# Moving a kernel's SBUF-to-DRAM-to-SBUF bounces from GpSimd's DMA queue to SyncE's, and estimating their loads as parallel

## The chip, the cores and the metric

The kernel runs on one core of a Trainium2 chip. The metric is device time in microseconds of one execution; three runs of the kernel before gave 746.6, 746.7 and 748.06 us, median 746.7. A core has five engines, each with an instruction order of its own: TensorE (PE, with its weight loads as PEld), VectorE (DVE), ScalarE (ACT), GpSimd (POOL) and SyncE (SP). Any of the last three can issue a DMA; an engine works through its instructions in order, so one that waits holds up those behind it.

## What is computed

Two decoder layers over a sequence of 256 tokens with 1024 features, in float32. Each layer is a token mixer with two attention branches, then a SwiGLU feed-forward, each followed by a layer norm over the scaled residual. Cut to its frame:

```python
def hybrid_mixer(x, w_in, w_branch_sb, w_branch_moba, w_out):
    proj = x @ w_in
    q_sb, k_sb, v_sb, q_mb, k_mb, v_mb, g_sb, g_mb = jnp.split(proj, cuts, axis=-1)
    o_sb = stick_breaking_attention(...)                       # 8 heads of 64
    o_mb = moba_attention(partial_rope(q_mb), partial_rope(k_mb), v_mb)   # 8 heads of 64
    merged = sigmoid(g_sb) * (o_sb @ w_branch_sb) + sigmoid(g_mb) * (o_mb @ w_branch_moba)
    return merged @ w_out

def swiglu(x, w_gate, w_up, w_down):                           # D_FF = 2816
    return (silu(x @ w_gate) * (x @ w_up)) @ w_down

for l in range(2):
    x = layer_norm(ALPHA * x + hybrid_mixer(x, ...))
    x = layer_norm(ALPHA * x + swiglu(x, ...))
```

With 256 tokens MoBA's block is the whole sequence, so that branch is causal softmax attention.

## The kernel before

**Weights.** They stream through SBUF once, as 2 x 122 granules of 128 x 1024 float32 (512 KB). For accuracy each granule is used as two parts, a rounded high part and the rest (`whi`, `wlo`), and each product is three matmuls (`mm3`: high x high, high x low, low x high, line 423; `mm` issues them at line 417). The parts lie in two rings of ten places; a place is free again when TensorE has used the granule ten before (`allow`).

Most granules are loaded by SyncE into one of six raw buffers (`load`, line 135), cast by ScalarE into `whi`, and subtracted by VectorE into `wlo`, which frees the raw buffer (`line`, lines 149 to 172). Seven granules of each layer (22, 25, 28, 31, 34, 37, 40, "soft") go another way, without VectorE: GpSimd issues a DMA from the weights straight into `whi` (`cast_line`), ScalarE writes the negative of that into `wlo`, and GpSimd issues a second DMA that adds the weights to it (`rest_line`).

**The order of the work.** The program is written out in one pass by a planner, `Weave`. TensorE's matmuls advance an estimated time `weave.t`. Everything else is a generator ("side") that yields the estimated time at which it may go on; after each group of matmuls, `tick` steps every side whose time has come, and what it issues is then next in that engine's order. Three helpers issue an instruction and estimate its end: `act` (line 47), `dve` (line 52), `pool` (line 57). Each holds a clock for its engine: an instruction begins at the later of that clock and `e`, the time at which its input is there, and the helper returns its end plus a hop of 0.21 us. In the trace all instructions that go through a helper carry the helper's line: L48 for ScalarE, L53 for VectorE, L58 for GpSimd. The soft granules' estimated arrival follows from the end that `pool` returns, and so does `ws.dma_t`, the estimate of when the DMA engines are free. These estimates decide only the order; on the chip every instruction waits on semaphores for what it really needs.

**The bounces.** The rotary query and key of the MoBA branch, and the first four feed-forward chunks, are computed with tokens on the partitions but needed with features there. `turned_line` (line 501) turns a 128 x (n x 128) tile: VectorE transposes its 32 x 32 blocks into `half`, one DMA stores `half` to a scratch tensor in DRAM (`scr`, three buffers of each size), and four DMAs load the blocks back rearranged, each into 32 partitions of `out`. The loads wait for the store's landing. With n = 4 (query and key: `l0qmb`, `l0kmb` and so on, two token halves each) a store has 256 KB and a load 64 KB; with n = 2 (`l0sg` into `l0hb`, four each layer) it is half of that. That makes eight bounces, eight stores and 32 loads, in each layer. GpSimd issues all of them. What comes back is split into two parts by ScalarE and VectorE (`split_line`).

**Stages of a layer,** in TensorE's order: MoBA query and stick-breaking value (`l0pv`, `l0pq`; `l1pvq`), query and key of stick-breaking heads (`l0pqk`) around the MoBA key (`l0pk`), MoBA value (`l0pu`), the gates (`l0pg`) with the attention's scores (`l0sb_s`, `l0mb_s`), transposes (`_pT`) and outputs (`_o`) in between, the branch projections (`l0pb`), the output projection (`l0pw`), the norm's transposes (`l0a_tp`), four feed-forward chunks (`l0pft`), the other eighteen (`l0pf`), and the down projection (`l0pd`, in the second layer `l1pd` and `l1pe`).

Of the kernel before, what the change touches and what calls it, by code (L numbers as in the profile page):

```python
# [34 lines left out]
class Weave:  # L35
# [16 lines left out]
    def dve(self, e, n, f, *args, **kw):  # L52
        f(*args, **kw)  # L53
        self.dve_t = max(self.dve_t, e) + n / 960.0 + DVE_FIXED
        return self.dve_t + HOP

    def pool(self, e, f, *args, **kw):
        f(*args, **kw)  # L58
        self.pool_t = max(self.pool_t, e) + 0.3
        return self.pool_t + HOP  # L60

    def add(self, gen, due=0.0, last=False):
# [36 lines left out]
class WeightStream:  # L99
# [5 lines left out]
    def __init__(self, nc, pool, rings, w, total, weave):  # L105
        self.nc, self.pool, self.rings, self.w, self.total, self.weave = nc, pool, rings, w, total, weave
        self.soft = [g for g in range(total) if SOFT(g)]
        self.hard = [g for g in range(total) if not SOFT(g)]
        self.loaded = self.split = self.cast = self.done = 0
        self.limit = NSPLIT - 1  # L110
        self.current = 0
        self.dma_t = 1.7
        self.raw, self.parts, self.there, self.ready = {}, {}, {}, {}
# [140 lines left out]
DMA_STORE = 3.0  # L254
DMA_LOAD = 3.0
# [3 lines left out]
def hybrid_trunk_kernel(ctx: ExitStack, tc: tile.TileContext, w, xT_in, x_in, ln_in,  # L259
                        ident_in, mask_in, rope_in, out):  # L260
    nc = tc.nc
# [54 lines left out]
    act, dve, pool = weave.act, weave.dve, weave.pool  # L316
# [73 lines left out]
    e = dve(3.6, 512, nc.vector.tensor_copy, hi, ws.raw[0][:, first[0]])  # L390
# [110 lines left out]
    def turned_line(name, out, half, src, n, e):  # L501

        scr = dram.tile([P, n * P], F32, tag=f"scr{n}", name=f"{name}_scr")
        e = dve(e, n * P, nc.vector.transpose, half.rearrange("p (j n b) -> p n j b", j=4, n=n),
                src.rearrange("p (n j a) -> p n j a", n=n, j=4))
        yield e
        e = pool(e, nc.gpsimd.dma_start, scr, half) + DMA_STORE
        yield e
        blocks = scr.rearrange("(i a) (j c) -> j a i c", a=32, j=4)
        for j in range(4):  # L510
            e = max(e, pool(e, nc.gpsimd.dma_start, out[32 * j:32 * j + 32].rearrange("a (i c) -> a i c", i=4),
                            blocks[j]) + DMA_LOAD)
        yield e
        return out.rearrange("p (i n b) -> p n i b", i=4, n=n), e

# [3 lines left out]
    def rope_line(name, ps, t, put, scale=1.0):  # L519

        both = unit(f"{name}_tok{t}", [P, 2, WIDTH])
        tmp = both[:, 0, :].rearrange("p (h d) -> p h d", d=DH)
        e = act(pe_done(), WIDTH, nc.scalar.activation, tmp, ps.rearrange("p (h d) -> p h d", d=DH), AF.Copy,
                scale=scale)
        yield e
        half = ROPE // 2
        a, b = (p.tile([P, n], F32, tag=tag, name=f"{name}_{tag}{t}")[:, :8 * ROPE]
                .rearrange("p (h r) -> p h r", h=8) for p, tag, n in ((page1, "ra", 240), (page2, "rb", 208)))
        cc = rope[:, t, 0, None, :].to_broadcast([P, 8, ROPE])
        s0 = rope[:, t, 1, None, :half].to_broadcast([P, 8, half])  # L530
        s1 = rope[:, t, 1, None, half:].to_broadcast([P, 8, half])
        mul = nc.vector.tensor_mul
        dve(e, P, mul, a, tmp[:, :, :ROPE], cc)
        dve(e, P // 2, mul, b[:, :, :half], tmp[:, :, half:ROPE], s0)
        dve(e, P // 2, mul, b[:, :, half:], tmp[:, :, :half], s1)
        e = dve(e, 2 * P, nc.vector.tensor_add, tmp[:, :, :ROPE], a, b)
        tp, e = yield from turned_line(f"{name}{t}", both[:, 0, :], both[:, 1, :], both[:, 0, :], NPAIR, e)
        yield from put(tp, slice(t * P, (t + 1) * P), e)
# [232 lines left out]
    for l in range(DEPTH):  # L771
# [112 lines left out]
        for c, b in ((0, 0), (1, 0), (0, 1), (1, 1), *((c, b) for c in range(2, KC) for b in range(2))):  # L884
# [15 lines left out]
            e = dve(0.0, S, nc.vector.tensor_add, mt[:, 0, :], mt[:, 0, :], mt[:, 1, :])  # L900
# [21 lines left out]
        def h_line(name, ps, j, t):  # L922
            sg = work.tile([P, 256], F32, tag="T", name=name)
            e = act(pe_done(), 256, nc.scalar.activation, sg, ps[:, :256], AF.Sigmoid)
            yield e
            dve(e, 256, nc.vector.tensor_mul, sg, sg, ps[:, :256])
            e = dve(e, 256, nc.vector.tensor_mul, sg, sg, ps[:, 256:])
            tp, e = yield from turned_line(name, hb[t][:, j, 1, :], hb[t][:, j, 0, :], sg, 2, e)
            ts = slice(t * P, (t + 1) * P)
            yield from split_line(*(blocked(h[:, 2 * j:2 * j + 2, ts]) for h in h_t[0]), tp, 256, e)  # L930
# [139 lines left out]
```

## Time and profile before

| what | value |
|---|---|
| median of three runs | 746.7 us (746.6 to 748.06) |
| profiled execution | 745.83 us |
| its span, first to last instruction | 744.0 us |
| PE busy | 718.3 us (97%) |
| PEld busy | 659.5 us (89%) |
| DVE busy | 524.7 us (71%) |
| ACT busy | 391.1 us (53%) |
| POOL busy | 77.9 us (10%), 128 instructions |
| DMA | 149.95 MB, 202 GB/s over the span |
| weight loads issued by SP | 226 of 512 KB, median 4.4 us to landing |
| soft granules' DMAs issued by POOL | 28 of 512 KB, median 4.5 us (high) and 7.4 us (low) to landing |

Times in the profile are microseconds from the span's start. In a timeline row stand start, length, engine, source line, operation, output and inputs, and in brackets how long the engine stood idle before it and what released it. In the list of waits stand the waiting instruction, what it waited for, the sum, the count and the longest. A DMA's row on SP or POOL is its issue; the landing comes later and is listed apart. The granted clock is TensorE's, as a share of full speed.

### The profile page before, as it was taken

The numbers are of one execution on the slowest core, as the hardware profiler recorded it, in microseconds if no ns is written. First come the engines' busy times: TensorE is split into PE (matmuls) and PEld (weight loads), VectorE is DVE, ScalarE is ACT, GpSimd is POOL, SyncE is SP. The second block draws the span as 40 slices with busy tenths as digits, with TensorE's granted clock in tenths as the row PEclk, the third lists the DMA queues.
The fourth block names the chain that finished last, engine by engine and source line by source line (L and its number), as shares of the span: only waits on it lengthen the run. The fifth ranks groups of instructions, "written<-read, shape, count | busy, mean of one in ns | idle before, by whom it ended". The sixth has DMA issues, their size and how long they took to land.

```text
span 744.0 us, 12787 instructions
## 1 busy us (share of the span) xinstructions
PE 718.3 (97%) x5032; PEld 659.5 (89%) x5032; DVE 524.7 (71%) x792; ACT 391.1 (53%) x588; POOL 77.9 (10%) x128
## 2 busy tenths in 40 slices
PE   8996899999999999999999999899999999999995
PEld 6986699998899999988889888799988999998884
DVE  5997568786896766644588887777679766665415
ACT  5756377754565545533356565686346545554300
POOL 0123011000230000000012221100012300000001
PEclk9999799999999999999999999999999999999998
DMA  8997677555597565566259486857636966563501
GB/s 304 357 317 238 154 199 209 183 176 171 200 306 239 189 199 199 171 241 218 72 191 344 159 223 175 214 159 244 195 113 224 314 197 201 182 197 100 230 1 57
DMA packets 45083, 149.95 MB, mean 202 GB/s; under 512 B 5984, under 2 KB 8032, under 8 KB 45024
## 3 DMA queue, kind: packets, MB, share of 16 engines
q1 hardware_dynamic: 37776, 127.91, 50.8%
q0 software_dynamic: 7104, 20.98, 11.7%
q8 instruction: 39, 0.64, 0.3%
q10 hardware_dynamic: 144, 0.26, 0.1%
q14 instruction: 20, 0.16, 0.1%
HBM read 144.93 MB, written 4.19 MB: 200 GB/s over the span
## 4 chain that ended last, share of the span: by engine, by line
PE 93%; ACT 2%; DMA 2%; DVE 2%; issue 0%; POOL 0%; POOLq 0%; SPq 0%; DVEq 0%
PE l1pf L417 13%; PE l0pf L417 13%; PE l0pd L417 8%; PE l0pg L417 6%; PE l1pg L417 6%; PE l1pe L417 4%; PE l1pd L417 4%; PE l1pqk L417 3%; PE l0pw L417 3%; PE l1pw L417 3%; PE l1pft L417 3%; PE l0pft L417 3%; PE l1pvq L417 3%; PE l0pb L417 3%; PE l0pqk L417 3%; PE l1pb L417 2%
## 5 line engine op out<-in xcount | busy, mean ns | idle before, releaser
L53 DVE TENSOR_TENSOR wlo<-raw,whi 128x1024 fp32r<-128x1024 f32 (+1 forms) x234 | 278.3, 1203 | 87.1 <-ACT whi L48 83.9
L48 ACT CAST whi<-raw 128x1024 fp32r<-128x1024 f32 (+1 forms) x233 | 238.4, 1036 | 84.4 <-PE l0pd L417 19.7
L417 PE MATMUL l1pf<-xT_hi,whi 128*128 128x256 f32 x288 | 79.6, 276 | 0.0
L417 PE MATMUL l1pf<-xT_hi,wlo 128*128 128x256 f32 x288 | 79.6, 276 | 0.0
L417 PE MATMUL l1pf<-xT_lo,whi 128*128 128x256 f32 x288 | 79.6, 276 | 0.0
L417 PE MATMUL l0pf<-xT_hi,whi 128*128 128x256 f32 x288 | 79.5, 276 | 0.0
L417 PE MATMUL l0pf<-xT_hi,wlo 128*128 128x256 f32 x288 | 79.5, 276 | 0.0
L417 PE MATMUL l0pf<-xT_lo,whi 128*128 128x256 f32 x288 | 79.5, 276 | 0.0
L417 PEld LDWEIGHTS l1pf<-xT_hi,whi 128*128 128x128 f32 x288 | 54.1, 188 | 0.0
L417 PEld LDWEIGHTS l1pf<-xT_lo,whi 128*128 128x128 f32 x288 | 54.1, 188 | 0.0
L417 PEld LDWEIGHTS l1pf<-xT_hi,wlo 128*128 128x128 f32 x288 | 54.1, 188 | 0.0
L417 PEld LDWEIGHTS l0pf<-xT_hi,whi 128*128 128x128 f32 x288 | 54.1, 188 | 0.0
L417 PEld LDWEIGHTS l0pf<-xT_lo,whi 128*128 128x128 f32 x288 | 54.1, 188 | 0.0
L417 PEld LDWEIGHTS l0pf<-xT_hi,wlo 128*128 128x128 f32 x288 | 54.1, 188 | 0.0
L417 PE MATMUL l1pg<-xT_hi,whi 128*128 128x256 f32 x128 | 36.5, 286 | 1.4 <-DVE l1vmb L53 1.4
L417 PE MATMUL l0pg<-xT_hi,whi 128*128 128x256 f32 x128 | 36.0, 281 | 0.0
L417 PE MATMUL l1pg<-xT_hi,wlo 128*128 128x256 f32 x128 | 35.9, 280 | 0.0
L417 PE MATMUL l1pg<-xT_lo,whi 128*128 128x256 f32 x128 | 35.9, 280 | 0.0
L417 PE MATMUL l0pg<-xT_hi,wlo 128*128 128x256 f32 x128 | 35.5, 277 | 0.0
L417 PE MATMUL l0pg<-xT_lo,whi 128*128 128x256 f32 x128 | 35.4, 277 | 0.0
L417 PE MATMUL l0pd<-whi,l0h_hi 128*128 128x512 f32 x88 | 34.5, 391 | 0.0
L417 PE MATMUL l0pd<-wlo,l0h_hi 128*128 128x512 f32 x88 | 34.3, 389 | 0.0
(359 smaller groups left out, 1841.3 us busy)
## 6 DMA issues: line engine op xcount, KB each, us to landing
raw<-in_w_dram SPq DMA_DIRECT2D x226, 512.0 KB, 4.4
whi<-in_w_dram POOLq DMA_DIRECT2D x14, 512.0 KB, 4.5
wlo<-in_w_dram POOLq DMA_DIRECT2D x14, 512.0 KB, 7.4
ln<-in_ln_dram SPq DMA_DIRECT2D x8, 512.0 KB, 5.4
raw<-in_w_dram SPq DMA_DIRECT2D x7, 256.0 KB, 5.7
x<-in_x_dram SPq DMA_DIRECT2D x2, 512.0 KB, 7.9
out_dram<-x SPq DMA_DIRECT2D x3, 256.0 KB, 2.0
xT_raw<-in_xT_dram SPq DMA_DIRECT2D x4, 128.0 KB, 4.1
```

What stands on the lines that cost most here:

```text
L48: f(*args, **kw)
L53: f(*args, **kw)
L417: nc.tensor.matmul(o, a, b, start=start, stop=stop)
```

## The change

The bounce's store and its four loads are issued by SyncE, whose queue otherwise holds the weight loads, instead of by GpSimd. In the planner's estimates they no longer occupy GpSimd; the store counts 3.0 us as before, and the four loads count as begun together, 3.0 + 2.0 us for all four, where before each was estimated to begin when the one ahead of it had landed. The estimate for any instruction that is still issued through `pool` rises from 0.3 to 0.55 us.

```diff
     def pool(self, e, f, *args, **kw):
         f(*args, **kw)
-        self.pool_t = max(self.pool_t, e) + 0.3
+        self.pool_t = max(self.pool_t, e) + 0.55
         return self.pool_t + HOP
...
         yield e
-        e = pool(e, nc.gpsimd.dma_start, scr, half) + DMA_STORE
+        nc.sync.dma_start(scr, half)
+        e += DMA_STORE
         yield e
         blocks = scr.rearrange("(i a) (j c) -> j a i c", a=32, j=4)
         for j in range(4):
-            e = max(e, pool(e, nc.gpsimd.dma_start, out[32 * j:32 * j + 32].rearrange("a (i c) -> a i c", i=4),
-                            blocks[j]) + DMA_LOAD)
+            nc.sync.dma_start(out[32 * j:32 * j + 32].rearrange("a (i c) -> a i c", i=4), blocks[j])
+        e += DMA_LOAD + 2.0
         yield e
```

## The prediction

> **What bounds the kernel now.** I read the page first, then the waits, then the timelines of the one place that the waits point to.
>
> ```profile
> span 744.0 us, 12787 instructions
> PE 718.3 (97%) x5032; PEld 659.5 (89%) x5032; DVE 524.7 (71%) x792; ACT 391.1 (53%) x588; POOL 77.9 (10%) x128
> PEclk9999799999999999999999999999999999999998
> PE l0pu L417 <- DMA wlo<-in_w_dram: 9.7, 1, 9.7
> PE l1mb_pT L430 <- DVE l1mb_e L53: 3.5, 1, 3.5
> PE l1pg L417 <- DVE l1vmb L53: 1.4, 1, 1.4
> ```
>
> TensorE works 718.3 of 744.0 us, so an edit of transfers can win only where TensorE stands still, or where its clock is low because it stood still. The waits name three such places: 9.7 us in the first layer and 3.5 and 1.4 us in the second. The fifth clock digit, a 7 among nines, lies just behind the first. The windows compare that stretch with its twin in the second layer, which does the same matmuls (the value projection l0pu or l1pu, half of the stick-breaking scores and two transposes):
>
> ```profile
> 65.00:91.00 26.00, 16.32 (x84) 13.06 (x82) 14.77 (x22) 10.92 (x16) 5.38 (x8) 0.80 0.78 216
> 432.70:448.20 15.50, 14.17 (x85) 11.42 (x83) 13.36 (x21) 10.20 (x14) 0.54 (x1) 1.00 0.85 250
> 78.00:82.00 4.00, 4.00 (x27) 3.12 (x27) 0.70 (x1) 0.52 (x1) 0.00 (x0) 0.50 1.06 268
> 79.13 2.86 PE l0sb_s L547 x16
> 408.68 1.57 PE l1sb_s L547 x24
> ```
>
> The columns are length, then busy time of PE, PEld, DVE, ACT, POOL, then granted clock and DMA share. The same work takes 26.0 us in the first layer and 15.5 in the second, where PE is busy 14.17 us at full clock. Of the 10.5 us more, 9.7 is the wait; behind it the clock is 0.50, and one block of scores takes 2.86 us instead of 1.57.
>
> What that wait is made of stands in the timelines of POOL and ACT. "whi" and "wlo" there are the seven granules of each layer (the first is granule 22) that are not loaded by SyncE: GpSimd loads the high part, ScalarE writes its negative into the low part, and GpSimd adds the weights to that by a second, accumulating DMA.
>
> ```profile
> 35.80 4.37 POOL L58 DMA_DIRECT2D l0qmb_tok<-l0qmb_scr  x8 [1.93 <-ACT whi L48]
> 46.23 0.56 POOL L58 DMA_DIRECT2D whi<-in_w_dram  x1 [6.06 <-PE l0pk L417]
> 62.80 4.35 POOL L58 DMA_DIRECT2D l0kmb_tok<-l0kmb_scr  x8
> 68.52 0.95 POOL L58 DMA_DIRECT2D wlo<-in_w_dram  x1 [1.37 <-ACT whi L48]
> 49.65 0.62 ACT L48 CAST l0qmb_hi<-l0qmb_tok 128x512 fp32r<-128x512 f32 x1
> 61.14 0.61 ACT L48 CAST l0qmb_hi<-l0qmb_tok 128x512 fp32r<-128x512 f32 x1
> 64.58 1.06 ACT L48 ACTIVATE wlo<-whi 128x1024 fp32r<-128x1024 f32 x1
> 77.91 0.79 PE L417 MATMUL l0pu<-wlo,xT_hi 128*128 128x512 f32 x1 [9.68 <-DMA wlo<-in_w_dram]
> ```
>
> Granule 22's high part is issued at 46.23, but ScalarE negates it only at 64.58, and GpSimd adds to it only at 68.52, behind eight loads of the bounce. TensorE needed it at 68.23 (77.91 less 9.68).
>
> **The change part by part.**
>
> *The estimates.* Today a bounce's four loads are estimated one behind the other, 0.3 + 0.21 + 3.0 us each, 14.0 us together, and each pushes the planner's GpSimd clock along. The query's two bounces put that clock some 25 us ahead (eight steps of 3.51 less the last landing), and the estimated arrival of granule 22 with it, so its negation is planned, and written into ScalarE's order, late. The trace bears this out: the two casts of l0qmb are written 11.5 us apart (49.65 and 61.14), though their loads were all issued from 35.80 to 40.17. After the change the four loads count 5.0 us together and nothing on GpSimd's clock; GpSimd's own steps count 0.55 instead of 0.3, which moves an estimate by 0.25 us a step and is costed at nothing. So granule 22 is planned from its issue on.
>
> ```profile
> L58 POOL DMA_DIRECT2D whi<-in_w_dram x1: 560/560/560, 46.2 to 46.2; - x1
> DMA to landing us min/median/max: 7.9/7.9/7.9
> L58 POOL DMA_DIRECT2D wlo<-in_w_dram x14: 849/878/997, 68.5 to 488.5; - x14
> DMA to landing us min/median/max: 5.4/7.4/12.0
> ```
>
> The chain becomes: issue 46.2 (it still waits for l0pk), landing 7.9 us later at 54.1, negation 1.06, some 0.3 to GpSimd, accumulating DMA 7.4 us (bounds 5.4 and 12.0): it lands at 62.9 (60.9 to 67.5). TensorE asks at 68.2, so even the slow end covers it, by 0.7 us; if ScalarE ends the negation later than 68.2 - 7.4 - 0.3 = 60.5, the cover is gone and the wait returns for the excess.
>
> *The stall's worth.* The 26.0 us become at best the 14.2 us of busy PE, a gain of 11.8. What is late next is the wait that the second layer shows at the same place (l1pg for VectorE's l1vmb, 1.4 us), because VectorE is loaded there (13.36 of 15.5 us, and 14.77 of work in the first layer's stretch). I take the twin's 15.5 us: a gain of 10.5. The lower bound adds to that the second layer's other wait, which could appear in the first as well: 3.5 us and the half clock behind it, so a gain of 5.4 at least.
>
> ```profile
> 468.00:473.00 5.00, 4.05 (x22) 4.06 (x23) 3.83 (x12) 4.46 (x13) 0.88 (x1) 0.66 0.91 283
> ```
>
> (Clock 0.66 over 5 us is 3.4 us at half; at most that lies in work, so some 1.6 us lost.)
>
> *GpSimd's queue.* It loses 16 stores and 64 loads of some 0.55 us, 44 of its 77.9 us, and no granule's DMA stands behind a bounce any more. Only the step above is on the path; the norms' four pairs on GpSimd come when it is idle. Costed at nothing beyond the 10.5.
>
> *SyncE's queue.* It takes the same 80 DMAs.
>
> ```profile
> 14.32 0.42 SPq L406 DMA_DIRECT2D ident<-in_ident_dram  x1
> L135 SPq DMA_DIRECT2D raw<-in_w_dram x226: 327/328/826, 7.8 to 695.2; - x113
> SPq L135 <- DVE wlo L53: 367.5, 150, 15.5
> l1sg_scr<-l1hb POOLq DMA_DIRECT2D x4, 128.0 KB, 4.1
> ACT l0sf L48 <- PE l0pf L417: 32.2, 18, 1.8
> ACT whi L48 <- DMA raw<-in_w_dram: 16.0, 15, 3.8
> ```
>
> The nearest row to a bounce load (rows of 512 bytes) is ident, 0.42 us, so 80 x 0.42 = 34 us more beside 226 x 0.33 = 75 us of weight loads: a queue that now spends 367.5 us waiting for raw buffers has room. New is a wait: the four loads wait on SyncE until their store has landed (4.1 us for l1sg), and the weight loads behind them wait too, for up to 4.1 + 4 x 0.42 = 5.8 us. Who waits for that is a ScalarE cast of a raw granule, and behind that cast ScalarE's other work. Such a cast waits 15 times already (16.0 us in all) and TensorE does not notice; in the feed-forward ScalarE waits 1.8 us a time for TensorE. So I take zero; the other bound is one full hold in each layer less that 1.8, 2 x 4.0 = 8 us.
>
> The bounce also joins the weight loads' queue. Of that the trace has no row; a landing is bounded by the least of l0sg's and by the raw loads' own (up to 9.5 us, further below).
>
> ```profile
> DMA to landing us min/median/max: 2.1/5.2/7.1
> 73.65 0.62 ACT L48 CAST l0kmb_hi<-l0kmb_tok 128x512 fp32r<-128x512 f32 x1 [2.31 <-DMA l0kmb_tok<-l0kmb_scr]
> 98.81 1.57 PE l0mb_s L547 x22
> ```
>
> What the bounces carry is used first by the MoBA scores at 98.8, 25 us behind its last cast, and comes sooner after the change. So for the attention stages I take zero beyond the twin's 1.4 us; the other end is the slower rival.
>
> *Sum.* 745.83 us is the profiled execution, 744.0 its span; it stands 0.9 us below the median of 746.7. 745.8 - 10.5 = 735.3; against the median **736.2, so 736 us**.
>
> The half clock's share of the gain comes from these windows:
>
> ```profile
> 72.00:74.00 2.00, 0.00 (x0) 0.00 (x0) 0.06 (x1) 0.35 (x1) 0.00 (x0) 0.71 1.05 279
> 82.00:84.00 2.00, 2.00 (x7) 1.63 (x8) 1.97 (x5) 1.70 (x3) 0.00 (x0) 0.73 0.71 139
> ```
>
> A mean of 0.71 over two microseconds puts the fall to 0.50 at 72.8, 4.6 us into the wait, and 0.73 puts the return at 83.1, 5.2 us after work resumed. [...]
>
> **The rivals.**
>
> *Only issue time is saved.* If ScalarE's order does not move, only the eight loads (4.35 us) leave GpSimd's queue: the add goes at 65.6 + 0.3 = 65.9 instead of 68.52, and the wait shrinks by 2.6: 744 us. For it: the row at 64.58, which is ScalarE's. Against it: the 11.5 us between the two casts, which come from the estimates that are changed. [...]
>
> *More is won.* The second layer's order moves too, and its waits of 3.5 and 1.4 us and the 1.6 us of half clock go: 736.2 - 6.5 = 730. They come from ScalarE and VectorE, not from a bounce; little speaks for it.
>
> *A wait moves in.* The removed 10.5 us come back elsewhere in the first layer as VectorE's lateness (it is busy 35.8 of 37.3 us before the stall): 746.7, no change.
>
> *Slower: turned halves arrive later than planned.* The casts of a bounce are now written 3.0 + 5.0 us behind its turning on VectorE, and ScalarE waits in order.
>
> ```profile
> L135 SPq DMA_DIRECT2D raw<-in_w_dram x10: 327/328/328, 30.0 to 46.6; - x10
> DMA to landing us min/median/max: 4.5/8.2/9.5
> 27.70:65.00 37.30, 37.30 (x285) 34.63 (x284) 35.78 (x62) 23.85 (x34) 10.65 (x20) 1.00 0.84 276
> 48.48 0.96 DVE L53 TENSOR_TENSOR l0sb_beta<-l0sb_beta,l0sb_inc 128x766 f32<-128x766 f32 x1
> L430 PE MATMUL l0sb_pT<-ident,l0sb_beta x12: 272/272/273, 50.6 to 53.9; 128*128 128x128 f32 x12
> ```
>
> From 30 to 57 us a load on SyncE's queue takes 8.2 us to land where the plan allows 5.0: ScalarE would stand 3.2 us, and TensorE's transposes at 50.6 have 1.2 us in hand over VectorE's end at 49.44. So 2.0 us a split, 16 us over the eight splits of both mixers: 752 us. It decides from 10.5 / 8 = 1.3 us lost per split, a landing at 7.5 us. Against it: in that stretch ScalarE is busy 23.85 of 37.3 us, so it has 13 us of its own to stand in.
>
> **How the numbers follow.** Stall gone, twin's pace: 0.57. More won: 0.11. Issue time only: 0.12. Wait moves in: 0.06. Slower: 0.14. A change within 0.2% (1.5 us) cannot be told from none. Faster is the first three, 0.80; same 0.06; slower 0.14. The range reaches from 729 (under the 730 case) to 745 (over the lower bound of the gain, 741, the 744 of the feed-forward's bound and the 744 case) and leaves out the last two cases; the likeliest one alone spans 735 to 741.
>
> **What would show it.** The wait of l0pu for wlo gone, the clock digit a 9, and the stretch from the first l0pu matmul to l0pg near 15 us; wlo negated before 60 us and added before 62; l0qmb's casts close together near 40 to 45; POOL near 34 us. Wrong would be: a PE wait behind ScalarE on a bounce's landing, or raw loads standing behind a bounce with a cast waiting for them.

## The result, and the profile after

| | before | after |
|---|---|---|
| median us (lowest to highest) | 747.11 (746.1 to 748.42) | 753.02 (748.4 to 757.88) |
| ratio after/before, 95% interval | | 1.0084 (1.0067 to 1.01) |
| profiled execution, its span | 745.83, 744.0 | 751.43, 749.6 |

The change made the kernel 0.8% slower, where 736 us was forecast. The times after also spread over 9.5 us, those of before over 2.3. Ratios here and below are of fast executions alone, which leaves out one of 767.18 us of the variant e1. The page after:

```profile
span 749.6 us, 12757 instructions
PE 723.9 (97%) x5032; PEld 664.0 (89%) x5032; DVE 524.6 (70%) x792; ACT 391.2 (52%) x590; POOL 33.5 (4%) x48
PEclk9999899899999999999999989999999999999999
```

```profile
l0kmb_scr<-l0kmb_tok SPq DMA_DIRECT2D x2, 256.0 KB, 5.6
l0kmb_tok<-l0kmb_scr SPq DMA_DIRECT2D x8, 64.0 KB, 6.8
```

The span grew by 5.6 us, and TensorE's busy time by the same 5.6 (718.3 to 723.9). So TensorE stands still as long as before (25.7 us in both); the same 5032 matmuls run slower. The clock has an 8 at three places now, for the one 7 of before (the 8 of its last slice aside). The two rows of the second fence, from the list of DMAs, end with the median time from issue to landing of the key's stores and of its loads: 5.6 + 6.8 = 12.4 us, where the plan now says 3.0 + 5.0.

What the change was forecast to do for granule 22, it did. GpSimd's timeline and ScalarE's show it:

```profile
54.13 0.89 POOL L58 DMA_DIRECT2D wlo<-in_w_dram  x1 [1.02 <-ACT wlo L48]
```

```profile
41.66 0.62 ACT L48 CAST l0qmb_hi<-l0qmb_tok 128x512 fp32r<-128x512 f32 x1 [1.33 <-DVE wlo L53]
45.35 0.62 ACT L48 CAST l0qmb_hi<-l0qmb_tok 128x512 fp32r<-128x512 f32 x1 [1.17 <-DMA l0qmb_tok<-l0qmb_scr]
...
52.78 1.06 ACT L48 ACTIVATE wlo<-whi 128x1024 fp32r<-128x1024 f32 x1
...
71.36 0.62 ACT L48 CAST l0kmb_hi<-l0kmb_tok 128x512 fp32r<-128x512 f32 x1 [5.88 <-DMA l0kmb_tok<-l0kmb_scr]
71.89 0.58 ACT L48 CAST l0qkhi<-l0pqk 128x512 fp32r<-128x512 f32 x1
```

Granule 22 is negated at 52.78 (before 64.58) and added at 54.13 (before 68.52), and TensorE's wait of 9.7 us is gone. The last two rows show what took its place. ScalarE stands 5.88 us for the key's bounce, and `l0qkhi`, whose input TensorE finished at 65.4 us, is written behind that cast. Before, `l0qkhi` stood ahead of it, at 65.54. The waits after, first ScalarE's for bounces, then TensorE's:

```profile
ACT l0h_hi L48 <- DMA l0hb<-l0sg_scr: 10.7, 4, 4.2
ACT l1h_hi L48 <- DMA l1hb<-l1sg_scr: 10.6, 4, 3.3
ACT l1kmb_hi L48 <- DMA l1kmb_tok<-l1kmb_scr: 6.9, 2, 4.2
ACT l0kmb_hi L48 <- DMA l0kmb_tok<-l0kmb_scr: 5.9, 1, 5.9
ACT l1qmb_hi L48 <- DMA l1qmb_tok<-l1qmb_scr: 2.9, 2, 2.1
ACT l0qmb_hi L48 <- DMA l0qmb_tok<-l0qmb_scr: 1.2, 1, 1.2
...
PE l0pu L417 <- DVE l0qklo L53: 4.0, 1, 4.0
PE l0mb_o L417 <- DVE pp L53: 3.2, 1, 3.2
PE l0pg L417 <- DVE l0vmb L53: 2.8, 1, 2.8
PE l1sb_s L548 <- ACT l1qkhi L48: 2.5, 1, 2.5
PE l0pf L417 <- ACT whi L48: 2.4, 1, 2.4
PE l1pf L417 <- DVE l1sf L53: 1.1, 1, 1.1
```

Columns are the sum, the count and the longest. ScalarE waits for a bounce at 14 of its 16 casts, 38.2 us in all; before it was 2 casts and 3.8 us. TensorE's one long wait has become six short ones, 16.0 us together. None of the releasers named for TensorE is a bounce; one has to follow the chain back. It runs through the first of these waits so:

```profile
55.88 6.27 DMA l0kmb_scr<-l0kmb_tok
...
64.02 7.28 DMA l0kmb_tok<-l0kmb_scr
...
71.36 0.63 ACT l0kmb_hi L48
...
72.74 0.70 DVE l0qklo L53
...
73.48 2.72 PE l0pu L417 x6
```

The store begins at 55.88 and the last load lands at 71.30, 15.4 us later. The cast follows, its rest on VectorE, then the rest of `l0qk`, which TensorE has wanted since 69.49 (73.48 less 4.00). The time from the end of the transpose on VectorE to the last landing, for all sixteen bounces of this run, lies between 9.1 and 16.0 us; in the run of before it lay between 8.1 and 19.8. Never was it as short as the 8.0 us of the plan.

The chains of l0pg, l0pf and l1sb_s lead back to a bounce in the same way. Two others do not. That of l1pf leads to a weight load on SyncE:

```profile
584.99 1.75 SPq L512 DMA_DIRECT2D l1hb<-l1sg_scr  x4
586.84 0.38 SPq L135 DMA_DIRECT2D raw<-in_w_dram  x1
```

The load stands behind a bounce's four loads, which went out only when their store, issued at 580.22, had landed; it lands at 589.9, its cast follows, and behind that come VectorE's steps that TensorE waits 1.1 us for. That of l0mb_o leads through work of ScalarE and VectorE back to TensorE itself, and to no bounce; the wait is still 2.5 us in e4 below, where no cast waits for one.

Most of the short waits have low clock behind them:

```profile
73.00:78.00 5.00, 4.51 (x30) 3.50 (x30) 2.97 (x5) 3.13 (x4) 0.85 (x1) 0.66 0.93 321
86.00:91.00 5.00, 4.28 (x23) 4.28 (x24) 1.27 (x3) 0.60 (x1) 0.00 (x0) 0.66 0.03 7
145.00:153.00 8.00, 6.25 (x30) 6.09 (x31) 3.98 (x9) 4.15 (x11) 0.00 (x0) 0.57 0.52 193
444.00:454.00 10.00, 7.15 (x27) 5.67 (x28) 7.61 (x12) 6.02 (x8) 0.00 (x0) 0.66 0.63 191
225.00:233.00 8.00, 7.48 (x65) 7.51 (x66) 7.93 (x12) 5.64 (x9) 0.00 (x0) 1.00 0.83 266
```

The clock column (before the DMA share) gives twice (1 - 0.66) x 5 = 3.4 us at half speed behind the waits of l0pu and l0pg, 6.9 us behind l0mb_o's and 6.8 us behind l1sb_s's: 20.5 us in all. Of that 2.4 us lie inside waits (the clock over the waits of 3.18, 2.46 and 0.49 us before 146.75, 446.36 and 447.33 is 0.79, 0.89 and 0.50). At full clock l0pu's matmuls start 0.23 us apart (65.22 to 69.10), at half 0.43 (73.86 to 75.57), nearly twice; taken as twice, 9.1 us are lost, by estimate. Before it was 10.3 + 3.4 us at half speed, 5.1 of them inside the long wait, so 4.3 lost. The difference of 4.8 is most of the 5.6 by which PE's busy time grew. The last row stands behind the wait of l0pf, and there the clock stayed full.

### The profile page after: what moved, and what is told of

It reads as the page before. It is cut to its first block, busy times and chain, and to the rows that moved or that the text cites. A ratio compares the mean times of both kernels' runs of the same rounds, so it can differ in the third digit from the quotient of the medians.

```text
span 749.6 us, 12757 instructions
## 1 busy us (share of the span) xinstructions
PE 723.9 (97%) x5032; PEld 664.0 (89%) x5032; DVE 524.6 (70%) x792; ACT 391.2 (52%) x590; POOL 33.5 (4%) x48
## 4 chain that ended last, share of the span: by engine, by line
PE 71%; DMA 11%; DVE 9%; SPq 3%; issue 2%; ACT 2%; POOL 1%; DVEq 0%; POOLq 0%; ACTq 0%
PE l0pf L417 12%; PE l1pf L417 12%; PE l0pd L417 8%; PE l0pg L417 6%; PE l1pg L417 6%; PE l1pe L417 4%; PE l1pd L417 4%; PE l0pb L417 3%; DVE wlo L53 3%; PE l1pb L417 3%; DMA raw<-in_w_dram 3%; PE l0pw L417 2%; PE l1pw L417 2%; SPq L512 2%; PE l1pvq L417 1%
```

## The experiments

Two theories stood at the start. **A, the order:** the casts are now written where a bounce of 8.0 us would have landed, and ScalarE, working in order, stands at each of them. **B, the queue:** SyncE's queue delays bounces or weight loads. Later runs ask how much the estimate is worth where, and how much the queue.

| run | median us (lowest to highest) | ratio to before | 95% interval |
|---|---|---|---|
| e1: estimates of after, GpSimd's queue | 762.28 (755.72 to 767.18) | 1.0177 | 1.013 to 1.0225 |
| e2: estimates of before, SyncE's queue | 739.58 (739.29 to 741.48) | 0.9908 | 0.9891 to 0.9925 |
| e3: loads 8.0 instead of 2.0 | 740.28 (735.9 to 742.2) | 0.9921 | 0.9899 to 0.9942 |
| e4: loads 14.0 | 730.82 (729.99 to 732.09) | 0.9787 | 0.977 to 0.9804 |
| e5: loads 14.0, GpSimd's queue | 735.57 (735.23 to 736.76) | 0.9853 | 0.9837 to 0.987 |
| e6: GpSimd's step 0.3 | 749.7 (747.51 to 753.25) | 1.0038 | 1.0018 to 1.0059 |
| e7: loads 14.0 in the mixers only | 739.51 (738.72 to 741.03) | 0.9905 | 0.9888 to 0.9921 |
| e8: loads 14.0 in the feed-forward only | 747.82 (743.25 to 754.02) | 1.0014 | 0.9991 to 1.0037 |
| e9: loads 14.0, GpSimd's step 0.3 | 730.08 (729.61 to 732.03) | 0.9779 | 0.9761 to 0.9797 |
| e10: loads 20.0 | 727.97 (727.78 to 728.87) | 0.9749 | 0.9733 to 0.9766 |

"Loads" is the constant added to `DMA_LOAD`, 2.0 in the changed kernel; a whole bounce is planned at 3.0 + 3.0 us and that, so at 8.0 there, 14.0 in e3, 20.0 in e4 and 26.0 in e10. The medians of the kernel before, run beside them, are 746.8 to 747.0 us.

**e1, the new estimates alone.** The changed kernel with the five DMAs back on GpSimd:

```diff
-        nc.sync.dma_start(scr, half)
+        nc.gpsimd.dma_start(scr, half)
...
-            nc.sync.dma_start(out[...]..., blocks[j])
+            nc.gpsimd.dma_start(out[...]..., blocks[j])
```

> The changed kernel's estimates (store 3.0 us, four loads 5.0 us together, GpSimd's clock not moved), but GpSimd issues the store and the loads again: the new order on the old queue. Theory A (order: ScalarE's casts of the turned tiles are written 8.0 us behind the turning, but the data lands 9 to 16 us behind it, so ScalarE stands and the work behind it is late): the waits of ScalarE on a bounce's landing stay or grow, 750 to 760 us. Theory B (queue: on SyncE the bounces and the weight loads hold each other up): without SyncE the cost goes and the gain from the earlier negation stays, 735 to 742 us.

762.28 us, 1.0177 (1.013 to 1.0225): slower still, and above A's 750 to 760. Its waits:

```profile
ACT l1h_hi L48 <- DMA l1hb<-l1sg_scr: 13.0, 4, 5.6
PE l0pg L417 <- DVE l0vmb L53: 9.5, 1, 9.5
PE l1pf L417 <- DVE l1sf L53: 4.4, 1, 4.4
```

The loss is there without a single bounce on SyncE, and larger: ScalarE stands 47.5 us for bounces, summed over the six groups of its list. So B is not the cause of the loss, and A has its sign. Not all of this run's loss is A's, though: beside the 9.5 us of l0pg its list has 6.3 us of ScalarE for the key's bounce and 1.5 us for the high part of a soft granule, where the run of after has 0.4. That on the old queue the bounces hold up the soft granules as well is my reading of these rows; e5 comes back to it.

**e2, the queue alone.** The estimates are those of before, the issuing engine is SyncE:

```diff
-        e = pool(e, nc.gpsimd.dma_start, scr, half) + DMA_STORE
+        e = pool(e, nc.sync.dma_start, scr, half) + DMA_STORE
...
-            e = max(e, pool(e, nc.gpsimd.dma_start, out[...]..., blocks[j]) + DMA_LOAD)
+            e = max(e, pool(e, nc.sync.dma_start, out[...]..., blocks[j]) + DMA_LOAD)
```

> The kernel before with all its estimates, only the store and the four loads issued by SyncE instead of GpSimd: the old order on the new queue. Theory A: no wait of ScalarE on a bounce that matters; TensorE's wait for the accumulated low part of granule 22 is shortened by up to 2.6 us, since no bounce stands before it on GpSimd: 742 to 747 us. Theory B: 749 to 756 us.

739.58 us, 0.9908 (0.9891 to 0.9925): a gain of 7.3 us, more than A expected, where B expected a loss. ScalarE's waits for raw granules and TensorE's wait for granule 22 in this run, then what became of that granule's add in the run of before and in this one:

```profile
ACT whi L48 <- DMA raw<-in_w_dram: 23.5, 17, 4.1
...
PE l0pu L417 <- DMA wlo<-in_w_dram: 4.0, 1, 4.0
```

```profile
L58 POOL DMA_DIRECT2D wlo<-in_w_dram x1: 949/949/949, 68.5 to 68.5; - x1
DMA to landing us min/median/max: 9.3/9.3/9.3
```

```profile
L58 POOL DMA_DIRECT2D wlo<-in_w_dram x1: 894/894/894, 66.3 to 66.3; - x1
DMA to landing us min/median/max: 6.3/6.3/6.3
```

TensorE's wait shrank by 5.65 us (9.68 to 4.03). The add is issued 2.2 us earlier, as the rival of issue time alone has it (2.6), and TensorE asks 0.4 later; the other 3.0 us are a landing of 6.3 instead of 9.3. That is most of the 6.6 us by which the span is shorter (744.0 to 737.4). That rival puts this run at 744 us, and the measured 739.58 is below it. Whether the landing is shorter because no bounce stood ahead of the add among GpSimd's transfers, or because other transfers ran beside it, no run here separates. ScalarE waits longer for raw granules (23.5 us against 16.0 before), and TensorE has no new wait from it.

**e3 and e4, a later plan.** In both only the loads' estimate of the changed kernel is raised:

```diff
-        e += DMA_LOAD + 2.0
+        e += DMA_LOAD + 8.0    # e3
+        e += DMA_LOAD + 14.0   # e4
```

> The changed kernel with the loads estimated at 3.0 + 8.0 us instead of 3.0 + 2.0, so that the casts are written 14.0 us behind the turning. Theory A: ScalarE's waits on a bounce's landing fall from some 39 us over the kernel to under 8, TensorE's waits behind them go, 735 to 742 us. Theory B: as the changed kernel, 749 to 757 us.

> The same with 3.0 + 14.0 us, casts written 20.0 us behind the turning, later than any landing seen (16.0 us in the changed kernel). Theory A: no ScalarE wait on a bounce at all, 734 to 742 us, and a spread of the runs as narrow as before (some 2 us). Theory B: 749 to 757 us.

e3: 740.28 us, 0.9921 (0.9899 to 0.9942), in A's range; ScalarE's waits for bounces are down to two:

```profile
ACT l1kmb_hi L48 <- DMA l1kmb_tok<-l1kmb_scr: 3.7, 1, 3.7
ACT l0kmb_hi L48 <- DMA l0kmb_tok<-l0kmb_scr: 1.7, 1, 1.7
```

e4: 730.82 us, 0.9787 (0.977 to 0.9804), below A's 734 to 742. No cast waits for a bounce, the clock's digits are all 9, and TensorE is busy 3.3 us less than before and 8.9 less than after:

```profile
PE 715.0 (98%) x5032; PEld 656.8 (90%) x5032; DVE 523.3 (72%) x792; ACT 392.8 (54%) x591; POOL 33.7 (5%) x48
PEclk9999999999999999999999999999999999999999
```

One constant is worth 22 us against the changed kernel, with the queue, the instructions' kinds and the bytes the same. The weight loads land no sooner (median 4.5 us, 4.4 after): it is the planned order alone that was edited. The two spans differ by 21.3 us (749.6 and 728.3), of which TensorE's work takes 8.9 and its standing still 12.4. Of the four waits whose chains led to a bounce, three are gone and l0pg's is down to 0.2 us, and l1pf's is gone too; so A is shown for these. The 2.5 us of l0mb_o stay, and come with the new order in some other way.

**e5, the right order on the old queue.** e4's estimate, the five DMAs back on GpSimd as in e1:

> As with 3.0 + 14.0 us, but GpSimd issues the store and the loads: the same estimates on the old queue. Theory A (only the order counts, and the queue is worth little once nothing waits for a landing): 730 to 735 us, no ScalarE wait on a bounce over 2 us, TensorE's waits under 7 us together. Rival C (the queue counts by itself, as the old order on the new queue gained 7 us: the bounces on GpSimd stand before the soft granules' DMAs): 737 to 746 us, with a wait of TensorE or ScalarE on an accumulated low part.

735.57 us, 0.9853 (0.9837 to 0.987), between the two expectations (730 to 735, and 737 to 746). The soft granules are late again: ScalarE waits 5.3 us for their high parts (2.6 in e4), and TensorE 2.0 us for work behind that, where before it waited 9.7 for granule 22. Rival C had named their low parts:

```profile
ACT wlo L48 <- DMA whi<-in_w_dram: 5.3, 3, 3.2
PE l0pg L417 <- DVE l0vmb L53: 2.0, 1, 2.0
```

So SyncE's queue is worth 0.9853 - 0.9787 = 0.7% or 4.9 us with this order, and 7.3 with the old one. It gains in both, and by e1 against the changed kernel (1.0177 and 1.0084) with the new estimates too.

**e6 and e9, the estimate of a GpSimd step.** e6 is the changed kernel, e9 is e4, each with 0.3 us a step again:

```diff
-        self.pool_t = max(self.pool_t, e) + 0.55
+        self.pool_t = max(self.pool_t, e) + 0.3
```

> The changed kernel with GpSimd's estimate back at 0.3 us instead of 0.55: the third part of the change undone alone. Theory A: the estimate of a step moves by 0.25 us and nothing else, so 749 to 757 us as the changed kernel. If it counted after all, a time outside of that.

> The run with 14.0 us for the loads, with the estimate of a GpSimd step back at 0.3 us instead of 0.55. If ScalarE's and VectorE's order around the bounces is what counts, the constant of a step moves nothing that can be seen: 729 to 733 us, beside 730.8. If the rise to 0.55 has a part in the gain (it plans the soft granules' negation and add a little later), 734 to 738 us and a wait of l0pu for wlo, or of ScalarE for whi.

e9 stands at 730.08, e4 at 730.82: no difference. e6 stands at 749.7 us, 1.0038 (1.0018 to 1.0059), in its range and with the same kinds of waits for bounces. Its interval does not touch the changed kernel's (1.0067 to 1.01), so with that order the step of 0.55 may cost some 3 us; the times of both spread widely, and no run settles it. It is not the main cause: with 0.3 the changed kernel is still some 10 us behind e2.

**e7 and e8, which half of a layer.** The estimate of 14.0 in the mixers' bounces only (n = 4), and in the feed-forward's only (n = 2):

```diff
-        e += DMA_LOAD + 2.0
+        e += DMA_LOAD + (14.0 if n == NPAIR else 2.0)   # e7
+        e += DMA_LOAD + (2.0 if n == NPAIR else 14.0)   # e8
```

> The changed kernel with 3.0 + 14.0 us for the query's and key's bounces alone (256 KB), and 3.0 + 2.0 us still for the feed-forward's. By the stages of the profiles, changed kernel against plus 14, the mixers hold some 17 of 21 us and the two feed-forwards 2.7 + 1.4: 733 to 738 us, ScalarE's waits on l0hb and l1hb as in the changed kernel (some 21 us together), those on the query's and key's tiles gone.

> The mirror: 3.0 + 14.0 us for the feed-forward's bounces alone (128 KB), 3.0 + 2.0 us for the query's and key's. 745 to 753 us, some 4 us under the changed kernel, with TensorE's waits in both mixers as there and none in the feed-forwards.

e7: 739.51 us, 0.9905 (0.9888 to 0.9921), 1.5 us above its range. What is left of its waits for bounces lies in the feed-forward, with one of the TensorE waits there:

```profile
ACT l1h_hi L48 <- DMA l1hb<-l1sg_scr: 12.6, 4, 5.3
ACT l0h_hi L48 <- DMA l0hb<-l0sg_scr: 11.8, 4, 3.9
...
PE l1pf L417 <- DVE l1sf L53: 2.4, 1, 2.4
```

e8: 747.82 us, 1.0014 (0.9991 to 1.0037), as expected; its waits lie in the mixers:

```profile
ACT l1kmb_hi L48 <- DMA l1kmb_tok<-l1kmb_scr: 13.0, 2, 8.4
PE l1sb_s L548 <- ACT l1qkhi L48: 8.6, 1, 8.6
```

The second row is the pattern of the first layer's `l0qkhi` again: scores of the stick-breaking branch, which use nothing of the bounce, stand behind the MoBA key's cast. From the changed kernel's 753.0, the mixers' bounces are worth 13.5 us, the feed-forward's 5.2, both together 22.2; the two are not quite additive.

**e10, later still.** `DMA_LOAD + 20.0`:

> The changed kernel with 20.0 us for the four loads instead of 2.0 (8.0 and 14.0 gave 740.3 and 730.8). In the run with 14.0 ScalarE never waited for a bounce. If the gain is only that no cast is written ahead of its landing, nothing is left to win: 729 to 734 us. If later planning still spreads VectorE's and ScalarE's work better, 722 to 728 us. If the casts now come too late for the MoBA scores or the feed-forward, TensorE waits behind them: 735 to 745 us, with new PE waits for l0kmb, l1kmb or l0h.

727.97 us, 0.9749 (0.9733 to 0.9766), in the range for later planning that still spreads the work better (722 to 728). It is below e4's 730.82 and, on the same chip, e9's 730.08, with ranges that do not touch. Nothing waited for a bounce in e4 already, so the reading that nothing is left to win missed, and ScalarE's standing is not all that the order costs. What TensorE still waits for:

```profile
PE l0pg L417 <- DVE l0vmb L53: 1.1, 1, 1.1
PE l0mb_o L417 <- DVE pp L53: 1.0, 1, 1.0
```

In e4 the second of these was 2.5 us, and two waits of the second layer (1.0 and 0.3 us) are gone. That later casts leave VectorE freer for the scores is an argument from these rows, not a test. This version is the fastest here and beats both kernels: 2.5% under the kernel before.

## Why the prediction was wrong

*The stall, right.* Estimates, issue, negation, add: granule 22 went as the steps say, the add at 54.13 us where the sum gives 55.5, the casts at 41.66 and 45.35 where 40 to 45 was forecast, GpSimd's busy time 33.5 us where 34 was. Two of the signs did not come: the fifth clock digit is an 8 and no 9, and the stretch from the first l0pu matmul (65.2) to l0pg (86.72) is 21.5 us and not 15, because new waits stand in it.

*SyncE's queue at zero, right on balance.* e2 and e5 put a gain on it. The weight loads do suffer, though after against before hides it (ScalarE's casts of raw granules wait 14.5 us against 16.0): with the estimates alike and only the queue changed, these waits rise from 16.0 to 23.5 us (before, e2), from 9.0 to 14.5 (e1, after) and from 15.0 to 25.4 (e5, e4). TensorE's wait of 1.1 us for l1pf is the one that I could follow back to this. The hold that was feared exists for the bounces themselves, too:

```profile
427.98 0.42 SPq L507 DMA_DIRECT2D l1kmb_scr<-l1kmb_tok  x1
435.51 1.75 SPq L512 DMA_DIRECT2D l1kmb_tok<-l1kmb_scr  x4
437.36 0.38 SPq L507 DMA_DIRECT2D l1kmb_scr<-l1kmb_tok  x1
```

The second half's store was ready at 429.12 us, when VectorE had turned it, and went out at 437.36, behind the first half's loads, which waited for their own store to land.

*"For the attention stages I take zero beyond the twin's 1.4 us": this step failed.* It asked when TensorE needs what the bounce carries (98.8 us, 25 us of slack) and concluded that an earlier cast can only help. The right question was what is written behind the cast on ScalarE. Those are `l0qkhi` and `l1qkhi`, which TensorE wants at once; 5.88 us of standing there cost TensorE 4.00. Measured against the zero, TensorE stands 13.0 us in the two mixers (4.0, 3.2, 2.8, 2.5 and 0.5), 9.8 of them behind a bounce's cast, and e7 gets 13.5 us back by the mixers' estimate alone. Both things that the prediction names as signs of being wrong came: a wait of TensorE behind ScalarE on a bounce's landing (l0pu), and a raw load behind a bounce with a cast waiting for it (l1pf). The "13 us of its own to stand in" were those of the stretch up to 65 us. There ScalarE stood 1.2 us for the query and TensorE not at all; the standing that cost came behind it, at one place.

*The rival called slower, right in mechanism, 752 us against 753.0 measured,* though held at 0.14. That the totals meet is luck, for the parts are others. It priced 2.0 us at each of eight casts of the mixers, from the query's place in the first layer, where TensorE did not wait at all, and it left the store at 3.0 us, which took 6.27 for the key. Measured, TensorE's waits come to 16.0 us, 3.5 of them in the feed-forward, which the rival left out, and TensorE's work takes 5.6 us more, mostly at half clock, which it left out too; on the other side the old waits of 3.5 and 1.4 us in the second layer are gone. The row that should have raised its chance stood in the prediction: the cast of l0kmb at 73.65, waiting 2.31 us for its load under the old estimate of 3.0 + 14.0 us. A cast that is late against 17 us will be late against 8.0.

*The 744 of issue time alone, too small a gain.* The queue alone is worth 7.3 us, since the add also lands 3.0 us faster.

*The size of the gain, possible after all.* With the order mended, e4 and e10 gain 16 and 19 us, more than the 10.5 of the stall and about the 16.7 of the case in which more is won. The change joined an edit that gains (the queue) to one that loses more (the estimate): the estimates take the ratio from 1 to 1.0177 on the old queue and from 0.9908 to 1.0084 on the new, some 13 us each.

## What to carry to other kernels

Where an order is planned from estimates and engines work in order, an estimate of a DMA that is too short is paid by whatever stands behind the waiting instruction, needed or not (here the key's bounce, planned at 8.0 us and landed 15.5 us behind its turning: 5.88 us of ScalarE, 4.00 of TensorE); one that was too long (a bounce planned at 26.0 us in e10) cost nothing here, as long as it moved no other work: before, the long estimates of the bounces had pushed granule 22 back. Measure the whole trip in the trace, from the producer's end to the last landing under the load of that stage, and plan with its worst. When a change moves work to another queue and also alters its estimate, time the two apart.

## What was not expected of the hardware

*A bounce's trip.* A store of 128 to 256 KB and four loads behind it take 8.1 to 19.8 us from GpSimd's queue (before) and 9.1 to 16.0 from SyncE's (after): two landings and the engine's own order between them.

*Half clock after short waits.* In the run of after, TensorE's waits of 3.18 us (l0mb_o, from 143.57) and 2.46 us (l1sb_s, with a second of 0.49 close behind) go with 6.9 and 6.8 us at half clock, those of 4.00 us (l0pu) and 2.8 us (l0pg) with 3.4 us each; the wait of 2.41 us before 225.52 brought none (the window from 225, clock 1.00). So in these rows the length of a wait does not tell what it costs in clock: the longest of them cost half of what the second longest did. What decides it, no run here tests.

*Spread.* The five kernels whose lists show ScalarE waiting for the second layer's key (after, e1, e3, e6 and e8, 3.7 to 13.0 us) vary by 5.7 to 10.8 us from one execution to the next (e1 by 7.1 without its 767.18), the other seven by 1.1 to 2.4. The sum of ScalarE's standing does not decide it: e7 waits 24.4 us for the feed-forward's bounces and varies by 2.3, e3 waits 5.4 and varies by 6.3. This is a pattern over twelve kernels; no run tests why.
